# Output projections of the FFNs and of cross attention: the second half as a Strassen pair group

## The chip, the cores and the metric

One core of a Trainium2 chip runs the whole program in one launch. Times are device microseconds of that core, and the kernel's time is the median of several executions. The engines named below are TensorE (PE), which multiplies matrices into PSUM; VectorE (DVE) and ScalarE (ACT), which work on tiles in SBUF and PSUM; GpSimd (POOL); and SyncE (SP), whose queue issues most of the DMAs.

## The reference

One layer of a streaming encoder in float32: 256 tokens, model width 2048, four post-norm blocks.

```python
D_MODEL, SEQ, D_FF, ALPHA = 2048, 256, 5504, 2.0 ** 0.25
def swiglu_ffn(x, w_in, w_out):
    g, u = jnp.split(x @ w_in, 2, axis=-1)
    return (jax.nn.silu(g) * u) @ w_out
...
def memory_cross_attention(h, mem, ...):
    ...
    o = jnp.einsum('bhqk,bkhd->bqhd', p, v).reshape(b, s, D_MODEL)
    return o @ w_xo
...
    h = layer_norm(ALPHA * h + 0.5 * swiglu_ffn(h, ffn1_w_in, ffn1_w_out), ln_ffn1_g, ln_ffn1_b)
    h = layer_norm(ALPHA * h + hybrid_mixer(h, ...), ln_mix_g, ln_mix_b)
    h = layer_norm(ALPHA * h + memory_cross_attention(h, mem, ...), ln_x_g, ln_x_b)
    h = layer_norm(ALPHA * h + 0.5 * swiglu_ffn(h, ffn2_w_in, ffn2_w_out), ln_ffn2_g, ln_ffn2_b)
```

The change touches three of these products, each with 2048 output columns: the two `@ w_out` of the FFNs (K = 5504, 43 tiles of 128) and `@ w_xo` (K = 2048, 16 tiles).

## The kernel before

**Number format.** Every fp32 operand is split into two planes of the type fp32r: `hi` is ScalarE's cast of the number (line 262 for weights), `lo` is what is left of it, subtracted on VectorE (line 265). A product takes three matmuls, hi by hi, hi by lo and lo by hi. The activations stand in SBUF with K on the partitions and are the stationary operand, 128 tokens at a time (a token half, `tt` is 0 or 1); the weights stream through, 512 columns a matmul.

**Weights.** `run()` works through a list of items. Each item has a function that issues matmuls or vector work, and the weights it needs. A weight tile of 2048 columns is 1 MB. It lands by a DMA of SP's queue in one of three `raw` buffers, ScalarE casts it in pieces of 1024 columns, and VectorE makes `lo` with one instruction. The planes go to one of two pairs of buffers ("units") or, where the item has tags, to named blocks of SBUF that happen to be free (X0 to X3, T0 to T3, H0 to H5). An item whose tags end in "early" may be loaded up to five weights ahead, others at most two, and only into a free unit.

**Two ways to multiply.** `out_proj` takes one block of 512 output columns at a time. For a group of four K tiles it issues, for each token half, 4 x 3 matmuls (`mm_tok`, line 296). `pair_group` takes two blocks of 512 columns together, as a 2 by 2 block product for two K tiles at a time: four PSUM tiles `ps[tt, a]`, one for each token half and column block. A plain step (`mm_pair`, line 309) is 2 x 2 x 2 x 3 = 24 matmuls. A step by Strassen's scheme (`mm_sums`, line 363) is seven products instead of eight, 7 x 3 = 21 matmuls. For it VectorE forms four sums of the weights' blocks (`weight_sums`, line 246 with 1024 columns and line 248 twice with 512), their planes take 2048 further columns in two blocks, and the raw tile's own planes need only 1536 of its 2048 columns. Four PSUM tiles `qs` collect products that several results share. At the end of the Strassen steps `shared` (lines 674 to 679) turns `qs` into four tiles in SBUF, which are added to the four results. The sums of the activations (`forms_step`) are kept in blocks named by SUMS_OUT and SUMS_XO and serve every column group.

**Around the change.** The FFN's hidden units are done in two parts of 24 and 19 K tiles (`F_SPLIT`). In the second part the output columns 0 to 1023 are a pair group (`out_pair`, with three Strassen steps, 3, 5 and 7) and the columns 1024 to 2047 are two blocks of `out_proj`, n = 2 and n = 3. The cross output has the same form: one pair group, then `out_proj` for n = 2 and 3. `finish` adds a PSUM tile to the residual `h` (line 749, or 747 with ALPHA) and takes its statistics for the layer norm (`bn_stats`, line 387).

**The skew.** The last four groups of n = 3 run through `skewed`: first all four for token half 0, then the same four, with the weights kept, for token half 1. While TensorE does the second round, the layer norm of half 0 runs on VectorE and ScalarE (`ln_scale`, `ln_T`, lines 392 to 427, 253 and 254), with transposes on TensorE (line 418). The next product starts with half 0 and is skewed likewise, over the layer norm of half 1. At the end of the program `final_steps` takes that place: half 0 is normalized and sent out during the second round, and the last group of half 1 is cut into two parts of 256 columns (`cut`), so that the last statistics wait for little.

**The order.** Instructions are put in order per engine by a scheduler at build time: among those that are ready by its own reckoning, the one that stands earliest in the program goes first, shifted by `prio` (SOON lifts an item by 400 places). On the chip each engine follows this order.

Of the kernel before, what the change touches and what calls it, by code (L numbers as in the profile page):

```python
# [36 lines left out]

AT_XQ = (4, 6), (2, 4, 6)
# [61 lines left out]
class Kernel:  # L100
# [450 lines left out]
    def ffn(self, tag, xT, st, first=None, steps=None, late=None, before=None, tags=None):  # L551
# [6 lines left out]
        for half, nf in enumerate(F_SPLIT):  # L558
# [33 lines left out]
            def out(hid=hid):  # L592
# [50 lines left out]
    def pair_group(self, bank, src, n, nk, x, at, fx, ps, qs, then=None, sums_in=SUM_HOME):  # L643


        steps = -(-nk // 2)
        sums = [c for c in range(steps) if c in at]
        for c in range(steps):
# [14 lines left out]
            def fn(w, c=c, kts=kts):  # L663
                if c == 0:
                    ps.update(self.group_tiles(bank))
                self.mm_pair(ps, w, n, x(), kts, c == 0, c == steps - 1)
# [88 lines left out]
    def out_proj(self, wname, nk, x, scale, st, steps=None, tags=None, n0=0, other=False, cut=False):  # L755
# [5 lines left out]
        groups = [list(range(i, min(i + 4, nk))) for i in range(0, nk, 4)]  # L761

        def finish(tt, n, ps):
            with self.prio(SOON if n == 3 and st is not None else 0):
                self.finish(tt, n, ps, scale, st)

        kept = {}

        def part(n, tts, i, ps, tags=None, held=0, keep=False, again=False):
            grp = groups[i]  # L770

            def fn(w=None):
                if keep:
                    kept[i] = w
                w = kept.pop(i) if again else w
                if cut and again and i == len(groups) - 1:
                    for a in range(2):
                        p = self.mm_tile()
                        self.mm_tok(p[:, :S], 1, w, x(), grp, True, True, a * S, S)
                        hs = h[1][:, n * 512 + a * S:n * 512 + a * S + S]  # L780
                        with self.prio(3 * SOON):
                            nc.vector.tensor_tensor(hs, hs, p[:, :S], ALU.add)
                            nc.vector.bn_stats(st[1][:, 3 + a, :], hs)
                    return
                for tt in tts:
                    if i == 0:
                        ps[tt] = self.at_tile() if other and n == n0 else self.mm_tile()
                    short = cut and again and i == len(groups) - 2
                    self.mm_tok(ps[tt], tt, w, x(), grp, i == 0, short or i == len(groups) - 1)
                    if short:  # L790
                        hs = h[tt][:, n * 512:(n + 1) * 512]
                        with self.prio(3 * SOON):
                            nc.vector.tensor_tensor(hs, hs, ps[tt], ALU.add)
                if i == len(groups) - 1:
                    for tt in tts:
                        finish(tt, n, ps[tt])
            ap = t[wname][n - n0, :, grp[0] * 512:(grp[0] + len(grp)) * 512]
            self.add(fn, *(() if again else ((ap, tags),)), held=held)

        last = len(groups) - 4  # L800
        for n in range(n0, 4):
            ps = {}
            for i in range(len(groups) if n < 3 or steps is None else last):
                part(n, (0, 1), i, ps)
        if steps is not None:
            self.skewed(lambda tt, j, **kw: part(3, (tt,), last + j, ps, **kw), steps(0), tags)
# [620 lines left out]
    def cross(self, xT, st, norm, steps_out):  # L1427
# [343 lines left out]
```

## Time and profile before

| what | value |
|---|---|
| device time, 3 runs | 2434.19 us median, 2432.38 to 2434.53 |
| profiled execution | span 2432.9 us, 29701 instructions; no separate time of it is on the page, its span lies inside the three runs |
| TensorE matmuls | 2423.0 us busy, 11286 instructions |
| TensorE weight loads | 2022.5 us (83%), beside the matmuls |
| VectorE | 2121.1 us (87%) |
| ScalarE | 1551.3 us (64%) |
| GpSimd | 36.1 us (1%) |
| DMA | 516.20 MB, mean 212 GB/s |

A timeline row gives start and duration in microseconds, engine, line, operation, result and operands, and a count of instructions merged into the row; in brackets stands the idle time of the engine before the row and what ended it. Durations of neighbouring instructions overlap a little, so the cost of one in a busy stretch is the distance from its start to the next start. A row of the stretches view gives a window, its length, and for each engine the busy time and in brackets the count.

### The profile page before, as it was taken

How to read it: one execution, taken by the hardware profiler on the slowest of the kernel's cores; microseconds unless marked ns; L12 is line 12 of the kernel's file. 1: busy time of each engine (PE TensorE's matmuls, PEld its weight loads, DVE VectorE, ACT ScalarE, POOL GpSimd, SP SyncE). 2: the span in 40 equal slices, each digit the busy share in tenths (PEclk: the TensorE clock that was granted, in tenths of full speed). 3: DMA queues.
4: the chain of work that ended last, by engine and by line, in shares of the span. 5: the costliest groups of instructions: out<-in, count | busy, mean ns of one | idle time of the engine just before them, and what ended most of it. 6: DMA issues, size and time to landing. Idle time of an engine off the chain costs nothing.

```text
span 2432.9 us, 29701 instructions
## 1 busy us (share of the span) xinstructions
PE 2423.0 (100%) x11286; PEld 2022.5 (83%) x11286; DVE 2121.1 (87%) x2423; ACT 1551.3 (64%) x2017; POOL 36.1 (1%) x81
## 2 busy tenths in 40 slices
PE   9999999999999999999999999999999999999999
PEld 8888888889888888888888888888888888888887
DVE  8999989899878898789788889979879999888997
ACT  6676745666555557878565687765666675556762
POOL 0000000000000001000000000000000000000000
PEclk9999999999999999999999999999999999999999
DMA  7766656666645657776577577655556666666665
GB/s 268 252 214 213 208 199 221 212 199 222 225 172 209 208 209 248 230 209 175 184 249 251 167 236 218 219 184 189 190 199 214 229 221 210 216 208 205 201 223 182
DMA packets 176414, 516.20 MB, mean 212 GB/s; under 512 B 111728, under 2 KB 112496, under 8 KB 121104
## 3 DMA queue, kind: packets, MB, share of 16 engines
q1 hardware_dynamic: 170816, 495.83, 61.2%
q0 software_dynamic: 4592, 17.30, 2.2%
q8 instruction: 88, 1.44, 0.2%
q10 hardware_dynamic: 864, 1.18, 0.1%
q14 instruction: 54, 0.44, 0.1%
HBM read 485.30 MB, written 2.10 MB: 200 GB/s over the span
## 4 chain that ended last, share of the span: by engine, by line
PE 90%; DVE 4%; ACT 3%; DMA 1%; issue 1%; SPq 0%; DVEq 0%; ACTq 0%
PE at L309 24%; PE mm L309 23%; PE mm L296 11%; PE at L363 10%; PE mm L363 10%; PE mm L275 5%; PE mm L277 2%; DVE lo L265 2%; ACT hi L262 1%; PE at L1028 1%; DMA raw<-w_xq 0%; PE at L1499 0%; PE at L1082 0%; PE at L275 0%; DMA raw<-w_o_b 0%
## 5 line engine op out<-in xcount | busy, mean ns | idle before, releaser
L262 ACT CAST hi<-raw 128x1024 fp32r<-128x1024 f32 (+1 forms) x852 | 805.3, 982 | 454.2 <-PE at L309 155.0
L265 DVE TENSOR_TENSOR lo<-raw,hi 128x2048 fp32r<-128x2048 f32 (+1 forms) x427 | 902.3, 2114 | 139.3 <-ACT hi L262 133.4
L309 PE MATMUL mm<-hi,T 128*128 128x512 f32 (+1 forms) x1328 | 311.1, 384 | 1.3 <-DVE v L397 1.3
L309 PEld LDWEIGHTS mm<-hi,T 128*128 128x128 f32 x1328 | 247.3, 188 | 48.5 <-DVE v L397 1.8
L309 PE MATMUL at<-hi,T 128*128 128x512 f32 x1152 | 275.5, 389 | 0.0
L262 ACT CAST X<-H 128x1024 fp32r<-128x1024 f32 (+1 forms) x166 | 170.6, 1034 | 162.0 <-DVE H L246 128.1
L309 PEld LDWEIGHTS at<-hi,T 128*128 128x128 f32 x1152 | 216.2, 188 | 45.1
L265 DVE TENSOR_TENSOR X<-H,X 128x2048 fp32r<-128x2048 f32 (+1 forms) x83 | 186.7, 2250 | 68.6 <-ACT X L262 68.6
L309 PE MATMUL mm<-lo,T 128*128 128x512 f32 (+1 forms) x664 | 160.4, 382 | 0.0
L309 PEld LDWEIGHTS mm<-lo,T 128*128 128x128 f32 x664 | 123.7, 188 | 22.8
L309 PE MATMUL at<-lo,T 128*128 128x512 f32 x576 | 142.4, 389 | 0.0
L309 PE MATMUL at<-hi,H 128*128 128x512 f32 x560 | 133.7, 389 | 0.0
L309 PEld LDWEIGHTS at<-lo,T 128*128 128x128 f32 x576 | 108.1, 188 | 22.5
L309 PEld LDWEIGHTS at<-hi,H 128*128 128x128 f32 x560 | 104.9, 188 | 21.6
L309 PE MATMUL mm<-hi,H 128*128 128x512 f32 x480 | 115.5, 391 | 0.3 <-DVE w L679 0.3
L248 DVE TENSOR_TENSOR H<-H,raw 128x512 f32<-128x512 f32 (+1 forms) x166 | 112.2, 676 | 2.2
L309 PEld LDWEIGHTS mm<-hi,H 128*128 128x128 f32 x480 | 89.5, 188 | 19.3 <-DVE w L679 0.8
L246 DVE TENSOR_TENSOR H<-raw 128x1024 f32<-128x1024 f32 (+1 forms) x83 | 99.4, 1198 | 0.9 <-DMA raw<-w_gate 0.8
L363 PE MATMUL mm<-X,X 128*128 128x512 f32 x342 | 91.1, 392 | 0.0
L262 ACT CAST X<-raw 128x1024 fp32r<-128x1024 f32 (+1 forms) x54 | 55.4, 1036 | 48.7 <-DVE raw L248 38.7
L363 PE MATMUL at<-X,X 128*128 128x512 f32 (+1 forms) x315 | 82.5, 386 | 0.9 <-DVE X L265 0.5
L849 ACT COPY w<-w 128x1024 uint16<-128x1024 uint16 (+1 forms) x60 | 75.8, 1276 | 0.6 <-DMA w<-w 0.5
(373 smaller groups left out, 4123.1 us busy)
## 6 DMA issues: line engine op xcount, KB each, us to landing
raw<-ffn_w_in SPq DMA_DIRECT2D x150, 1024.0 KB, 4.8
raw<-ffn_w_out SPq DMA_DIRECT2D x66, 1024.0 KB, 4.8
raw<-w_gate SPq DMA_DIRECT2D x32, 1024.0 KB, 4.8
raw<-ffn_w_out_r SPq DMA_DIRECT2D x16, 1024.0 KB, 4.9
raw<-w_qk SPq DMA_DIRECT2D x16, 1024.0 KB, 5.5
raw<-w_o_b SPq DMA_DIRECT2D x16, 1024.0 KB, 4.8
raw<-w_out SPq DMA_DIRECT2D x16, 1024.0 KB, 5.2
raw<-w_xk SPq DMA_DIRECT2D x16, 1024.0 KB, 5.3
```

Source lines behind the costliest of these rows:

```text
L246: self.nc.vector.tensor_tensor(two[0], two[1], raw[:, :m].unsqueeze(1).to_broadcast([P, 2, m]), ALU.add)
L248: self.nc.vector.tensor_tensor(t[:, a * m:a * m + m], t[:, b * m:b * m + m], raw[:, a * m:a * m + m], ALU.add)
L262: self.last_hi = self.nc.scalar.copy(hi[:, c:d], src[:, c:d])
L265: self.last_lo = self.nc.vector.tensor_tensor(lo[:, :n], src, hi[:, :n].bitcast(F32), ALU.subtract)
L275: self.nc.tensor.matmul(ps, hi[j], x.both(kt), start=(j == 0), stop=False)
L277: self.last_mm = self.nc.tensor.matmul(ps[:, :S], lo[j], x.at(0, kt), start=False, stop=(j == n - 1))
L296: self.last_mm = self.nc.tensor.matmul(ps, x.at(xi, kt)[:, tt * P:(tt + 1) * P], w[wi][:, j * 512 + c:j * 512 + c + m], start=(start and j ...
L309: self.last_mm = self.nc.tensor.matmul(ps[tt, g][:, :n], x.at(xi, kt)[:, tt * P:(tt + 1) * P], w[wi][:, c:c + n], start=first and j + wi + ...
L363: self.last_mm = self.nc.tensor.matmul(bank[:, :m], a[xi], v[wi][:, c * m:(c + 1) * m], start=own and first and wi + xi == 0, stop=own and ...
L849: self.nc.scalar.copy(self.words(u, n).rearrange("p (c k) -> p k c", k=2), self.words(s, n).rearrange("p (k c) -> p k c", k=2))
L1028: nc.tensor.matmul(ps[:, c0:c0 + nk], q[:, tt * P:(tt + 1) * P], k[:, :nk], start=(j == 0), stop=(j == len(parts) - 1))
```

## The change

The columns 1024 to 2047 of the three outputs become a second pair group for a part of the K tiles, with steps in a given order. The last eight K tiles of it stay out of the pair group: for them `out_skew` adds matmuls of the `out_proj` kind onto the same four PSUM tiles, token half 0 first (both column blocks), then token half 1. In the FFNs the order of steps is 6, 3, 8, 5, 9, 7, of which 3, 5 and 7 are Strassen steps and 9 has one K tile. In the cross output it is 0, 4, 2, 6 with 4 and 6 by Strassen. The sums of the activations that the first group used are used again. Weights are laid out to match on the host, with the same number of bytes.

The skew's four weight tiles in the cross output go to other blocks: H0 and H1, X0 and X1, T2 and T3, and T0 and T1, the last of them without "early"; before they went to T0 and T1, T2 and T3, H0 and H1, H2 and H3. In the final steps the gain of the third column block of token half 1 is applied after that block's `finish` (`self.tail`) instead of ahead of the second round.

```diff
+OUT_ORDER, OUT_ENDS = (6, 3, 8, 5, 9, 7), (0, 1, 2, 3, 4, 5, 8, 9)
+AT_XO, XO_ORDER, XO_ENDS = (4, 6), (0, 4, 2, 6), (2, 3, 6, 7, 10, 11, 14, 15)
...
-                    self.out_proj(tag + "_w_out_r", nf, x, False, st, steps, tags, 2, cut=tags is None)
+                    self.out_skew(bank ^ 1, src[1], tag + "_w_out_r", nf, OUT_ORDER, OUT_ENDS, x, homes, fh, False, st, steps,
+                                  tags, tags is None, SUM_HOME + ("H5",))
...
-    def pair_group(self, bank, src, n, nk, x, at, fx, ps, qs, then=None, sums_in=SUM_HOME):
+    def pair_group(self, bank, src, n, nk, x, at, fx, ps, qs, then=None, sums_in=SUM_HOME, order=None, open_end=False):
...
+        order = range(-(-nk // 2)) if order is None else order
+        sums = [c for c in order if c in at]
+        for i, c in enumerate(order):
...
-    def out_proj(self, wname, nk, x, scale, st, steps=None, tags=None, n0=0, other=False, cut=False):
+    def out_skew(self, bank, src, wname, nk, order, ends, x, at, fx, scale, st, steps, tags=None, cut=False,
+                 sums_in=SUM_HOME):
+        nc, t, h = self.nc, self.t, self.h
+        ps, qs, kept = {}, {}, {}
+
+        def shared():
+            for (tt, a), s in qs["add"].items():
+                hs = h[tt][:, (2 + a) * 512:(3 + a) * 512]
+                if scale:
+                    nc.vector.scalar_tensor_tensor(hs, hs, ALPHA, s, ALU.mult, ALU.add)
+                else:
+                    nc.vector.tensor_tensor(hs, hs, s, ALU.add)
+
+        def part(tt, j, tags=None, held=0, keep=False, again=False):
+            a, i = divmod(j, 2)
+            grp = ends[4 * i:4 * i + 4]
+
+            def fn(w=None):
+                if keep:
+                    kept[j] = w
+                w = kept.pop(j) if again else w
+                n, p = 2 + a, ps[tt, a]
+                if cut and tt and a and i:
+                    for b in range(2):
+                        p = self.mm_tile()
+                        self.mm_tok(p[:, :S], 1, w, x(), grp, True, True, b * S, S)
...
+                short = cut and tt and a
+                self.mm_tok(p, tt, w, x(), grp, False, short or i == 1)
...
+                elif i:
+                    with self.prio(SOON):
+                        self.finish(tt, n, p, False, st)
+                        if cut and tt:
+                            self.tail()
+            ap = t[wname][a, :, 2048 * i:2048 * i + 2048]
+            self.add(fn, *(() if again else ((ap, tags),)), held=held)
+
+        self.pair_group(bank, src, 512, nk, x, at, fx, ps, qs, shared, sums_in, order, True)
+        self.skewed(part, steps(0), tags)
...
-            self.out_proj("w_xo_r", KT, x, True, st, steps_out, (
-                ("T0", "T1", "early"), ("T2", "T3", "early"), ("H0", "H1", "early"), ("H2", "H3", "early")), 2)
+            self.out_skew(0, t["w_xo"][1], "w_xo_r", KT, XO_ORDER, XO_ENDS, x, AT_XO, fx, True, st, steps_out, (
+                ("H0", "H1", "early"), ("X0", "X1", "early"), ("T2", "T3", "early"), ("T0", "T1")), sums_in=(("T0", "T1"),))
...
-            for q in range(3):
-                hs = h[1][:, q * 512:(q + 1) * 512]
-                nc.vector.tensor_tensor(hs, hs, e["gb"][0][:, q * 512:(q + 1) * 512], ALU.mult)
+            for q in range(2):
+                gain(q)
+            self.tail = lambda: gain(2)
```

More of the change, by code (lines that the diff above doesn't have):

```diff
@@ L772, in fn @@
             def fn(w=None):
                 if keep:
[L774 to L777, printed above, removed]
+                    kept[j] = w
[3 more added lines that the diff above has]
+                    for b in range(2):
                         p = self.mm_tile()
-                        self.mm_tok(p[:, :S], 1, w, x(), grp, True, True, a * S, S)
-                        hs = h[1][:, n * 512 + a * S:n * 512 + a * S + S]
+                        self.mm_tok(p[:, :S], 1, w, x(), grp, True, True, b * S, S)
+                        hs = h[1][:, n * 512 + b * S:n * 512 + b * S + S]
@@ L781, in fn @@
                         with self.prio(3 * SOON):
                             nc.vector.tensor_tensor(hs, hs, p[:, :S], ALU.add)
-                            nc.vector.bn_stats(st[1][:, 3 + a, :], hs)
+                            nc.vector.bn_stats(st[1][:, 3 + b, :], hs)
                     return
[L785 to L797, printed above, removed]
-            self.add(fn, *(() if again else ((ap, tags),)), held=held)
[L800 to L806, printed above, removed]
+                short = cut and tt and a
```

32 lines of the change are left out of this document (16 added, 16 removed).

## The prediction

> **What bounds the kernel now.** I read the page's first two parts, then its chain, then the timelines of TensorE and VectorE around the three places, and last the busy time by stretches there.
>
> ```profile
> PE 2423.0 (100%) x11286; PEld 2022.5 (83%) x11286; DVE 2121.1 (87%) x2423; ACT 1551.3 (64%) x2017; POOL 36.1 (1%) x81
> PE 90%; DVE 4%; ACT 3%; DMA 1%; issue 1%; SPq 0%; DVEq 0%; ACTq 0%
> ```
>
> TensorE is the bound: it holds 90% of the chain that ended last and hardly ever waits. VectorE is second with 87%, an average over stages, so the question is how much of its 13% lies where the change puts work.
>
> ```profile
> 601.44 3.79 PE L309 MATMUL at<-hi,H 128*128 128x512 f32 x16
> ...
> 606.88 0.62 PE L363 MATMUL at<-hi,H 128*128 128x512 f32 x2
> ...
> 611.64 3.79 PE L309 MATMUL at<-hi,H 128*128 128x512 f32 x16
> ```
>
> This is the first FFN's existing pair group. A plain step starts at 601.44 and the next, a Strassen step, at 606.88: 24 matmuls in 5.44 us, 0.2267 us each. The Strassen step ends at 611.64: 21 matmuls in 4.76 us. One Strassen step is worth 0.68 us of TensorE, if nothing else changes.
>
> **TensorE's saving.** In each FFN n = 2 and 3 are 19 K tiles x 2 halves x 2 blocks x 3 = 228 matmuls. After: steps 24 + 21 + 24 + 21 + 12 + 21 = 123, and 8 x 2 x 2 x 3 = 96 for the last eight K tiles, 219 together. In the cross output 192 become 24 + 21 + 24 + 21 + 96 = 186. So 9 + 9 + 6 = 24 matmuls go, 24 x 0.2267 = 5.44 us (2.04, 2.04 and 1.36).
>
> The Trainium skill, TensorE: Matmul & The Clock Gate, Part 1, puts a warm matmul of 512 columns at about 215.7 ns; by that the saving would be an estimated 5.18 us. The rows say 226.7 ns at a granted clock of 1.00, and they decide.
>
> The second half-round is 48 matmuls after (two blocks x 8 K tiles x 3) and 45 or 48 before, so the cover over the layer norm of half 0 stays about 10.9 us. In the last product the cut group has four K tiles instead of three.
>
> ```profile
> 2418.21 5.04 PE L296 MATMUL mm<-X,H 128*128 128x512 f32 x30
> 2423.08 1.02 PE L1607 MATMUL mm<-h,ident 128*128 128x512 f32 x2
> ```
>
> The 30 are 12 of 512 columns (2.72 us) and 18 of 256, which leaves 2.15 us, 0.12 us each, so two halves cost about one whole and the longer cut is free to within 0.1 us.
>
> **What VectorE pays for a Strassen step.**
>
> ```profile
> 607.37 2.29 DVE L265 TENSOR_TENSOR X<-H,X 128x2048 fp32r<-128x2048 f32 x1 [1.12 <-ACT X L262]
> 609.58 2.28 DVE L265 TENSOR_TENSOR lo<-raw,hi 128x2048 fp32r<-128x2048 f32 x1
> 611.78 1.22 DVE L246 TENSOR_TENSOR H<-raw 128x1024 f32<-128x1024 f32 x1
> 612.91 1.75 DVE L265 TENSOR_TENSOR lo<-raw,hi 128x1536 fp32r<-128x1536 f32 x1
> 614.58 0.68 DVE L248 TENSOR_TENSOR H<-H,raw 128x512 f32<-128x512 f32 x1
> 615.18 0.55 DVE L254 TENSOR_TENSOR H<-w,H 128x384 fp32r<-128x384 f32 x1
> ```
>
> From start to start: `lo` of a plain tile 2.20 us; a Strassen step takes 2.21 (`lo` of the sums) + 1.13 (first sum) + 1.67 (`lo` of 1536 columns) + 2 x 0.60 (two more sums) = 6.2 us. Extra: 4.0 us of VectorE for 0.68 us of TensorE. ScalarE pays 1536 more columns, one and a half casts of about 1 us; with 64% busy I cost that at nothing, and without the slack it would be 12 us over eight steps.
>
> ```profile
> 621.91 0.68 DVE L676 TENSOR_TENSOR w<-w,mm 128x512 f32<-128x512 f32 x1
> 622.51 1.22 DVE L265 TENSOR_TENSOR lo<-raw,hi 128x1024 fp32r<-128x1024 f32 x1
> 623.64 0.69 DVE L677 TENSOR_TENSOR w<-w,w 128x512 f32<-128x512 f32 x1
> 624.25 0.68 DVE L628 TENSOR_TENSOR h<-h,w 128x512 f32<-128x512 f32 x1
> ...
> 627.85 2.29 DVE L265 TENSOR_TENSOR lo<-raw,hi 128x2048 fp32r<-128x2048 f32 x1
> 630.05 1.28 DVE L749 TENSOR_TENSOR h<-h,at 128x512 f32<-128x512 f32 x2
> ```
>
> Each new group also runs `shared` and its four additions to `h`: eight instructions at 0.60 to 0.62 us, 4.9 us. `finish` keeps its four additions and four statistics, only later. So VectorE gets 3 x 4.0 + 4.9 = 16.9 us in each FFN, 2 x 4.0 + 4.9 = 12.9 us in the cross output, 46.7 us in all.
>
> **Where that lands.** A weight can be prepared only one or two steps ahead: two units, three raw buffers, one home for the sums. So I take stretches that begin where VectorE has become continuously busy ahead of the place, and end where its work was last due.
>
> ```profile
> core 0: us, PE busy (x) PEld busy (x) DVE busy (x) ACT busy (x) POOL busy (x), PEclk, DMA share, GB/s
> 617.50:697.20 79.70, 79.00 (x365) 65.31 (x363) 64.44 (x83) 41.80 (x56) 0.00 (x0) 1.00 0.60 212
> 1675.30:1757.20 81.90, 81.90 (x378) 67.79 (x377) 73.36 (x96) 48.02 (x62) 0.00 (x0) 1.00 0.57 206
> 2359.00:2423.00 64.00, 64.00 (x292) 53.32 (x292) 50.41 (x59) 21.87 (x24) 0.00 (x0) 1.00 0.57 201
> 710.00:731.00 21.00, 21.00 (x94) 17.41 (x93) 11.38 (x15) 9.20 (x12) 0.16 (x1) 1.00 0.61 207
> ```
>
> FFN 1: VectorE has 64.44 of 79.70 us to do and gets 16.9 more: 81.3 us, so the stretch ends at least 1.6 us later than now, while TensorE alone would end 2.04 us earlier. Cross: 73.36 + 12.9 = 86.3 us in a stretch of 81.90, 4.4 us later. FFN 2: 50.41 + 16.9 = 67.3 us against 64.00, 3.3 us later. The ends are real due times:
>
> ```profile
> 695.89 1.29 DVE L254 TENSOR_TENSOR T<-w,T 128x512 fp32r<-128x512 f32 x2 [0.25 <-ACT T L253]
> 697.16 2.07 PE L296 MATMUL mm<-hi,T 128*128 128x512 f32 x8
> 1755.31 1.29 DVE L254 TENSOR_TENSOR T<-w,T 128x512 fp32r<-128x512 f32 x2 [0.25 <-ACT T L253]
> 1756.55 2.09 PE L296 MATMUL mm<-hi,T 128*128 128x512 f32 x8
> ```
>
> In both stretches the normalized half 1 is finished by VectorE just as TensorE starts on it; there is no lead left to spend. What VectorE did early inside the stretches (three of the next product's weights, 2.2 us each) is still due inside them.
>
> **FFN 2's end.**
>
> ```profile
> 2414.42 0.26 DVE L392 BATCH_NORM_AGGREGATE mv<-bn 128x2 f32<-128x24 f32 x1
> 2418.99 2.73 DVE L1596 SCALAR_TENSOR_TENSOR h<-h,y,T 128x512 f32<-128x512 f32 x4
> 2421.64 0.68 DVE L793 TENSOR_TENSOR h<-h,mm 128x512 f32<-128x512 f32 x1
> ```
>
> The norm of half 0 keeps VectorE busy from 2414.42 to 2421.64, when the last chain begins. `finish` of half 1's third block and its gain (two instructions of 0.6 us, one statistic) move into that time; they are no new work and count in the 64 us, but push the same chain.
>
> **Smaller edits.** The first Strassen step now comes second in its group, and its `qs` tiles are the PSUM that `finish` of the first group must empty: in FFN 1 the additions started at 630.05, and TensorE would want the tiles from 635.44 + 4 x 0.2267 = 636.3 on. Behind 6.2 us for the step's own weights they come up to 2.5 us late; bound 0 to 2.5 us a place. I take 0 on top, since VectorE works on meanwhile and the sum above already counts that work. In the cross output the layer norm writes T0, which the last weight tile now holds until 4 matmuls (0.9 us) before the round's end: bound 0 to 1.2 us (a cast and a subtraction of 512 columns, 0.6 us each). I take 0, because VectorE's backlog reaches that point later anyway; without the backlog it would be the 1.2 us. SP's queue issues the same bytes. In the cross output a Strassen step holds two of the three raw buffers, so a load starts later by up to its landing time:
>
> ```profile
> raw<-ffn_w_out SPq DMA_DIRECT2D x66, 1024.0 KB, 4.8
> ```
>
> With 4.8 us to land against 5.44 us a step this is bounded by 0 and about 2 us; I take 0, covered by the same backlog.
>
> **Sum.** 1.6 + 4.4 + 3.3 = +9.3 us, TensorE's 5.44 us being lost in waits for VectorE. The span of the profiled execution is 2432.9 us and the median 2434.19, 1.3 us above; on the median 2434.2 + 9.3 = 2443.5, I say 2443.
>
> **Rivals.**
>
> *The saving arrives.* VectorE carries its backlog out of the stretches into time where it is free: from 710 to 731 it is busy 11.38 of 21 us. Then 2434.2 - 5.4 = 2428.8, with a few tenths of waits 2429. It needs the norms' instructions to pass the carried weights without delaying them. Against it: the carried weights are those TensorE wants next. It decides if less than 0.6 us of the three overruns stays.
>
> *The FFNs come out as TensorE alone would have it, the cross output overruns.* In FFN 1 only 1.6 us are missing, and at the end some output work of half 0 can slide behind the last chain. -2.04 - 2.04 + 4.4 = +0.3: 2434.5.
>
> *The free time cannot be filled.* The three stretches have 15.3 + 8.5 + 13.6 = 37.4 us free. Part is latency: 1.12 us before line 265 above wait for ScalarE's cast. If a quarter stays free: 9.3 + 9.3 = +18.6, 2453; with a sixth, 2449.5.
>
> *TensorE slows down after long waits.* Its longest waits now are short, and the granted clock is 1.00 in all four stretches.
>
> ```profile
> PE mm L309 <- DVE v L397: 1.3, 1, 1.3
> ```
>
> If each overrun stood in one piece and matmuls ran at half rate for as long as the longest of them, 4.4 us, each place would lose 2.2 us more: 9.3 + 6.6 = +15.9, 2450. The Trainium skill, TensorE: Matmul & The Clock Gate, Part 1, has such a rule: an idle window of about 3.4 us halves the clock until it has been busy as long again. By it, an estimated 1.7 us is lost at a place; no row here shows a wait that long.
>
> **How the numbers follow.** A measurement of this kernel can tell about 0.2%, 4.9 us, from no change: 2429.3 and 2439.1 are the bounds. Chances: the sum 0.50 (its own range 2438 to 2448), the saving 0.12, the mixed case 0.25, unfilled time 0.10, the slow clock 0.03. The time is that of the likeliest, 2443. The range reaches from the saving, 2429.5, to unfilled time, 2453. Faster 0.10 (most of the saving's case), same 0.30 (the mixed case and edges of its neighbours), slower 0.60.
>
> **What would show it.** Right: 24 fewer matmuls and 2.04, 1.36 and 2.04 us less of TensorE's own time; VectorE busy above 97% from the first group's end through the layer norm at all three places, with about 47 us more in total; TensorE waiting there for line 265, line 749 or the norm's lines; the first `mm<-hi,T` on half 1 some 2 us later than now in FFN 1 and 4 us in cross. Wrong: VectorE with several free microseconds in those stretches while TensorE runs through; or weights prepared before the stretches begin, which the buffers should prevent.

## The result, and the profile after

| | median us | lowest to highest | runs |
|---|---|---|---|
| before | 2434.36 | 2432.38 to 2434.87 | 4 |
| after | 2464.36 | 2463.99 to 2465.01 | 4 |

The ratio is 1.0125, with a 95% interval of 1.0113 to 1.0137: 30 us slower, where 9 were forecast. The span of the profiled execution went from 2432.9 to 2462.2 us. Line numbers are two to six higher than before (296 became 298, 265 became 267, 418 became 420, 410 became 412, 1611 became 1617). First the engines and the chain on the page of after:

```profile
PE 2428.9 (99%) x11265; PEld 2021.4 (82%) x11265; DVE 2164.6 (88%) x2479; ACT 1564.9 (64%) x2037; POOL 35.9 (1%) x81
PE 86%; DVE 6%; ACT 3%; DMA 3%; issue 2%; SPq 0%; DVEq 0%; ACTq 0%
```

TensorE has 21 matmul records less, 24 for the Strassen steps and three more because the cut group splits 12 matmuls in two instead of 9. It is nevertheless 5.9 us busier: some of its work ran slower. VectorE has 43.5 us more, close to the 46.7 forecast. TensorE's share of the chain fell from 90% to 86%. What it waits for, by the waits of TensorE (total, times, longest):

```profile
PE at L420 <- DVE h L412: 6.8, 1, 6.8
PE at L420 <- issue: 5.8, 1, 5.8
PE mm L1617 <- ACT w L1615: 5.3, 1, 5.3
PE mm L298 <- DVE T L256: 2.5, 2, 2.2
PE mm L298 <- ACT T L255: 1.9, 2, 1.2
```

Three single long waits, one a place: in front of the transposes of half 0 in cross and in FFN 1, and in front of the program's last six matmuls. The timeline of VectorE in FFN 1 shows what happened ahead of the second:

```profile
678.55 0.24 DVE L394 BATCH_NORM_AGGREGATE mv<-bn 128x2 f32<-128x24 f32 x1
...
679.32 2.28 DVE L267 TENSOR_TENSOR lo<-raw,hi 128x2048 fp32r<-128x2048 f32 x1
681.51 0.14 DVE L374 TENSOR_SCALAR y<-v 128x1 int32<-128x1 int32 x1
682.13 0.69 DVE L752 TENSOR_TENSOR h<-h,mm 128x512 f32<-128x512 f32 x1 [0.47 <-PE mm L298]
...
683.82 2.23 DVE L267 TENSOR_TENSOR H<-raw,H 128x2048 fp32r<-128x2048 f32 x1
...
687.20 1.00 DVE L412 TENSOR_SCALAR h<-h,mv,y 128x512 f32<-128x512 f32 x2
```

Before, the same norm ran in one piece, by VectorE's timeline:

```profile
677.44 0.26 DVE L392 BATCH_NORM_AGGREGATE mv<-bn 128x2 f32<-128x24 f32 x1
...
679.86 1.00 DVE L410 TENSOR_SCALAR h<-h,mv,y 128x512 f32<-128x512 f32 x2
```

The aggregate is 1.1 us later, but from it to the scaling of half 0 it takes 8.65 us instead of 2.42: two remainders (`lo`) of the next product's weights and half 1's own additions and statistics stand between the norm's nine tiny, dependent instructions. Before, TensorE's transposes stood within its second round, in FFN 1 and in cross:

```profile
680.50 1.06 PE L418 MATMUL at<-ident,h 128*128 128x128 f32 x8 [0.70 <-issue]
...
1739.44 1.03 PE L418 MATMUL at<-ident,h 128*128 128x128 f32 x8
```

TensorE's timeline after:

```profile
687.84 3.46 PE L420 MATMUL at<-ident,h 128*128 128x128 f32 x16 [5.75 <-issue]
...
1758.83 3.67 PE L420 MATMUL at<-ident,h 128*128 128x128 f32 x16 [6.78 <-DVE h L412]
...
1765.86 3.12 PE L298 MATMUL mm<-hi,T 128*128 128x512 f32 x7 [2.24 <-DVE T L256]
...
2446.59 1.02 PE L1613 MATMUL mm<-h,ident 128*128 128x512 f32 x2
2452.95 2.08 PE L1617 MATMUL mm<-T,w 128*128 128x512 f32 x2 [5.34 <-ACT w L1615]
2454.82 1.92 PE L1617 MATMUL at<-T,w 128*128 128x512 f32 x2
2456.53 1.91 PE L1617 MATMUL mm<-T,w 128*128 128x512 f32 x2
```

Behind each long wait the same instructions are slow: a pair of 512 columns 1.9 to 2.1 us instead of 1.02. The stretches of after (window, length, busy time by engine, then the granted clock) show both:

```profile
617.99:705.73 87.74, 79.81 (x355) 64.51 (x354) 80.33 (x103) 47.02 (x63) 0.00 (x0) 0.96 0.55 197
1684.00:1779.90 95.90, 85.21 (x371) 68.54 (x369) 84.67 (x112) 51.27 (x68) 0.00 (x0) 0.95 0.52 178
2381.40:2446.00 64.60, 64.37 (x290) 52.16 (x290) 62.06 (x67) 27.50 (x31) 0.00 (x0) 1.00 0.51 186
```

VectorE's work came out as summed in FFN 1 (80.33 against 81.3 us) and in cross (84.67 against 86.3), yet it stands free there for 7.4 and 11.2 us. In FFN 2 it is 62.06 against 67.3: the end of half 0's norm, some 5 us of VectorE's work, now falls behind the stretch (its last row stood at 2418.99 before):

```profile
2443.53 0.26 DVE L394 BATCH_NORM_AGGREGATE mv<-bn 128x2 f32<-128x24 f32 x1
...
2449.34 2.73 DVE L1602 SCALAR_TENSOR_TENSOR h<-h,y,T 128x512 f32<-128x512 f32 x4
```

A finer cut in FFN 1:

```profile
680.00:690.00 10.00, 4.25 (x20) 3.58 (x19) 9.39 (x26) 2.90 (x5) 0.00 (x0) 0.71 0.62 215
690.00:700.00 10.00, 8.54 (x38) 6.85 (x38) 7.97 (x14) 7.45 (x15) 0.00 (x0) 0.95 0.01 5
```

The granted clock falls to 0.71 in the stretch with the wait of 5.75 us; in the 3.46 us of the transposes behind it it is 0.55, and 0.50 in cross's 3.67 us and in the last six matmuls. The Trainium skill, TensorE: Matmul & The Clock Gate, Part 1, says that an idle window of about 3.4 us halves the clock; this trace agrees for its three waits of 5.3 to 6.8 us.

To place the loss I use three marks: the first matmul on the normalized half 1 in FFN 1 (697.16 us before) and in cross (1756.55), and the end (2432.9). From mark to mark, after against before: FFN 1 +8.6, cross +14.8, FFN 2 +5.9, together 29.3 us. In FFN 1 the transposes start 7.3 us late (680.50 before) and the way from there to the mark takes 1.2 us more. In cross that is 10.8 and 4.0. In FFN 2 the last product ends 1.6 us *earlier* by the marks (2444.87 against 2423.08, with 23.4 us brought along), so TensorE's saving of 2.04 us nearly arrives, and the tail behind it takes 17.3 us instead of 9.8.

### The profile page after: what moved, and what is told of

It reads as the page before. It is cut to its first block, busy times and chain, and to the rows that moved or that the text cites. A ratio compares the mean times of both kernels' runs of the same rounds, so it can differ in the third digit from the quotient of the medians.

```text
span 2462.2 us, 29751 instructions
## 1 busy us (share of the span) xinstructions
PE 2428.9 (99%) x11265; PEld 2021.4 (82%) x11265; DVE 2164.6 (88%) x2479; ACT 1564.9 (64%) x2037; POOL 35.9 (1%) x81
## 4 chain that ended last, share of the span: by engine, by line
PE 86%; DVE 6%; ACT 3%; DMA 3%; issue 2%; SPq 0%; DVEq 0%; ACTq 0%
PE at L311 25%; PE mm L311 24%; PE at L365 11%; PE mm L365 11%; PE mm L298 6%; PE mm L277 5%; PE mm L279 2%; DVE lo L267 2%; ACT hi L264 1%; PE at L1030 1%; DMA raw<-w_xq 1%; DMA raw<-w_xv 0%; PE at L1501 0%; PE at L1084 0%; PE at L277 0%
## 5 line engine op out<-in xcount | busy, mean ns | idle before, releaser
L264 ACT CAST X<-H 128x1024 fp32r<-128x1024 f32 (+1 forms) x178 | 183.2, 1035 | 164.3 <-DVE H L248 128.6
L267 DVE TENSOR_TENSOR X<-H,X 128x2048 fp32r<-128x2048 f32 (+1 forms) x89 | 200.5, 2253 | 71.6 <-ACT X L264 71.6
L311 PE MATMUL mm<-hi,H 128*128 128x512 f32 x592 | 143.7, 391 | 0.4 <-DVE w L682 0.4
L311 PEld LDWEIGHTS mm<-hi,H 128*128 128x128 f32 x592 | 110.6, 188 | 23.7 <-DVE w L682 0.8
L250 DVE TENSOR_TENSOR H<-H,raw 128x512 f32<-128x512 f32 (+1 forms) x178 | 120.7, 678 | 2.3
L248 DVE TENSOR_TENSOR H<-raw 128x1024 f32<-128x1024 f32 (+1 forms) x89 | 106.8, 1200 | 1.4 <-DMA raw<-w_gate 1.0
L365 PE MATMUL at<-X,X 128*128 128x512 f32 (+1 forms) x369 | 98.0, 388 | 1.3 <-DVE X L267 0.7
L264 ACT CAST X<-raw 128x1024 fp32r<-128x1024 f32 x56 | 58.2, 1052 | 47.5 <-DVE raw L250 38.9
L365 PEld LDWEIGHTS at<-X,X 128*128 128x128 f32 x369 | 67.7, 188 | 17.9 <-DVE X L267 2.9
```

What stands on the lines that cost most here:

```text
L248: self.nc.vector.tensor_tensor(two[0], two[1], raw[:, :m].unsqueeze(1).to_broadcast([P, 2, m]), ALU.add)
L250: self.nc.vector.tensor_tensor(t[:, a * m:a * m + m], t[:, b * m:b * m + m], raw[:, a * m:a * m + m], ALU.add)
L264: self.last_hi = self.nc.scalar.copy(hi[:, c:d], src[:, c:d])
L267: self.last_lo = self.nc.vector.tensor_tensor(lo[:, :n], src, hi[:, :n].bitcast(F32), ALU.subtract)
L311: self.last_mm = self.nc.tensor.matmul(ps[tt, g][:, :n], x.at(xi, kt)[:, tt * P:(tt + 1) * P], w[wi][:, c:c + n], start=first and j + wi + ...
L365: self.last_mm = self.nc.tensor.matmul(bank[:, :m], a[xi], v[wi][:, c * m:(c + 1) * m], start=own and first and wi + xi == 0, stop=own and ...
```

## The experiments

The theories, by the letters of the expectations: A, VectorE has more to do than fits, and its backlog is the cause; B, the new form itself costs; C, the skew is lost because TensorE takes half 1's first products ahead of half 0's last; D, half 0's norm is cut open by the next product's weights; E, TensorE runs at half rate after a long wait. The table gives all runs; the last three columns are microseconds lost against before from mark to mark in the one profiled execution.

| kernel | median us | ratio, 95% interval | FFN 1 | cross | FFN 2 |
|---|---|---|---|---|---|
| after | 2464.36 | 1.0113 to 1.0137 | 8.6 | 14.8 | 5.9 |
| plain | 2437.28 | 1.0001 to 1.0019 | -0.1 | 2.8 | 1.2 |
| order | 2462.81 | 1.0097 to 1.0128 | 8.6 | 12.0 | 7.2 |
| hold | 2451.66 | 1.0048 to 1.0082 | 4.0 | 8.7 | 5.8 |
| warm | 2467.39 | 1.0117 to 1.0148 | 10.5 | 16.8 | 5.4 |
| homes | 2453.16 | 1.0062 to 1.0089 | 3.1 | 10.4 | 5.7 |
| hold_pool | 2463.09 | 1.0104 to 1.0132 | 9.3 | 13.4 | 7.6 |
| warm3 | 2462.39 | 1.0102 to 1.0129 | 9.6 | 12.1 | 5.9 |
| end | 2462.85 | 1.0102 to 1.0130 | 8.5 | 14.6 | 4.1 |
| light | 2442.59 | 1.0023 to 1.0051 | -0.8 | 9.4 | -0.4 |
| one_early | 2445.51 | 1.0037 to 1.0063 | 1.7 | 4.9 | 1.7 |
| one_late | 2445.97 | 1.0036 to 1.0064 | 2.0 | 10.3 | 1.9 |
| plain_load | 2469.83 | 1.0129 to 1.0160 | 14.5 | 13.6 | 7.8 |
| light_hold | 2438.98 | 1.0010 to 1.0027 | -0.3 | 4.9 | 0.9 |

**plain: the new form without its Strassen steps.**

```diff
-        self.pair_group(bank, src, 512, nk, x, at, fx, ps, qs, shared, sums_in, order, True)
+        self.pair_group(bank, src, 512, nk, x, (), fx, ps, qs, shared, sums_in, order, True)
...
-                        self.finish(tt, n, p, False, st)
+                        self.finish(tt, n, p, scale, st)
...
```

> The second groups keep the new form (two column blocks together, the given order of steps, eight K tiles by token halves, the new blocks for weights), but none of their steps goes by Strassen: 24 matmuls more, and VectorE loses the extra 46.7 us. Theory A (VectorE's extra work and what it holds up is the whole cause): back to the time before, 2434 us within 3 us, the layer norm of half 0 again inside the second half-round. Theory B (the form itself costs, for instance the blocks given to the last weights or the first group's PSUM wanted one step earlier): stays above 2445 us.

2437.28 us, at the edge of what A expected. The pair group, the order of K, the new blocks and the later `finish` cost about 0.1% (0.2% at most), most of it in cross; 27 of the 30 us belong to the Strassen steps.

**order: TensorE must finish half 0's products first.**

```diff
+                with self.tc.issue_after(kept["last"].ins) if tt else nullcontext():
                     self.mm_tok(p, tt, w, x(), grp, False, short or i == 1)
+                if not tt:
+                    kept["last"] = self.last_mm
```

> As the changed kernel, but TensorE must do all of token half 0's last matmuls before half 1's. In the changed kernel 17 to 24 of half 1's matmuls went ahead in each place because the last two weights of half 0 came late, so the norm of half 0 had about 7 us of matmuls over it instead of 10.9. Theory C (the lost skew is what costs): the cover is back, 10 us or more gained, about 2452 us. Theory A (VectorE is behind whatever TensorE does first): the wait only moves ahead, 2464 us within 3 us.

2462.81 us: the same. TensorE now waits for half 0's last weights (5.2 us at the longest, at line 267's remainder) and less for the norm. Theory C falls: TensorE's order was a consequence of late weights, not a cause. The transposes show something else here, by TensorE's timeline:

```profile
688.77 1.94 PE L420 MATMUL at<-ident,h 128*128 128x128 f32 x16 [1.58 <-issue]
...
1758.26 1.97 PE L420 MATMUL at<-ident,h 128*128 128x128 f32 x16 [2.88 <-DVE h L412]
```

In after the same transposes take 3.46 and 3.67 us. Here the granted clock is 1.00, and they follow the first scaling of `h` as closely as there (0.65 and 0.59 us behind it, against 0.64 and 0.60).

**hold: the next product's weights are prepared only behind half 0's norm** (FFN 1 and cross).

```diff
-            while nxt < len(queue) and ahead(need, held):
+            passed += fn is Kernel.wall
+            while nxt < len(queue) and (nxt < need or walls[nxt] <= passed) and ahead(need, held):
...
-        self.skewed(part, steps(0), tags)
+        first, *rest = steps(0)
+        self.skewed(part, [first if cut else first + [Kernel.wall], *rest], tags)
```

> As the changed kernel, but in FFN 1 and the cross output the next product's weights are loaded only once the norm of half 0 has been put into the program, so VectorE's subtractions for them stand behind that norm's chain. Same work, same matmuls. Theory D (the norm's chain of small instructions is cut open by two subtractions of 2.2 us, and TensorE waits for its end): the waits of 5.8 and 6.8 us in front of the transposes shrink to 1 or 2 us, with the slow clock behind them, about 2448 us. Theory A (the sum of VectorE's work decides): the same work comes later and TensorE waits for the weights instead, 2464 us within 4 us.

2451.66 us, 12.7 less than after. In FFN 1 the transposes stand inside the round again, by TensorE's timeline of this kernel, but the next weights are now late themselves:

```profile
680.44 0.63 PE L429 MATMUL at<-ident,h 128*128 128x128 f32 x4
...
691.05 1.20 PE L307 MATMUL mm<-lo,T 128*128 128x512 f32 x4 [0.61 <-DVE lo L276]
...
695.75 1.21 PE L307 MATMUL mm<-H,T 128*128 128x512 f32 x4 [1.67 <-DVE H L276]
```

So the early work on the next weights costs 4.5 us in FFN 1 and about 6 in cross, and putting it off turns a part of the loss into waits for the work put off, as A would have it. The cut norm is not all of the gain: from aggregate to scaling the norm takes 3.4 us in both places (8.7 and 8.5 in after), but the aggregate itself also comes 2.2 us (FFN 1) and 6.6 us (cross) sooner than in after.

**warm and warm3: 24 useless matmuls where TensorE would wait.** In warm the scheduler put them behind the transposes; in warm3 they write the tile of the first transposes and so stand in front of them; the norm's later steps also move behind the round.

```diff
+            if (tt, q) == (0, 0) and ln in ("ln_ffn1", "ln_x"):
+                x = self.warm_of[ln]()
+                with self.tc.issue_after(self.last_mm.ins):
+                    for _ in range(24):
+                        self.nc.tensor.matmul(ps, x.at(0, 0)[:, :P], x.both(0), start=True, stop=True)
...
```

> As the changed kernel, with 24 matmuls of 512 columns (5.4 us) of no use put behind the last matmul of FFN 1's and of the cross output's second half-round, where TensorE waits 5.8 and 6.8 us. Theory E (part of the loss is TensorE at half rate after a wait longer than some 3.4 us): the granted clock stays at 1.0 there, the 16 transposes take 1.6 us again instead of 3.5 and 3.7, and 4 to 5 us are gained in the two places, about 2459 us. If the clock costs nothing beside the wait: 2464 us or, where the extra matmuls outlast the wait, a little more.

> 24 useless matmuls of 512 columns (5.4 us) on TensorE between the last matmul of half 1 and the first transposes of half 0, in FFN 1 and in cross, so that TensorE does not stand still there. Theory E (TensorE runs at half rate after a wait of more than some 3 us): the 16 transposes take 1.6 us again instead of 3.46 and 3.67 and cross's next matmuls their 0.2267 us each; -1.9 and -3.8 us, less what the dummies overhang (up to 0.5 us in FFN 1): 2458.5 to 2460. Rival (the transposes are slow because each waits for VectorE's or ScalarE's next quarter of h): same time, 2464 to 2465, and the transposes stay at 3.4 us.

warm, 2467.39 us, tells nothing on the clock: the waits of 3.6 and 6.1 us stayed in front of the transposes, which stayed slow. warm3, TensorE's timeline:

```profile
681.91 5.61 PE L420 MATMUL at<-H 128*128 128x512 f32 x24
687.36 1.91 PE L425 MATMUL at<-ident,h 128*128 128x128 f32 x16
692.35 3.83 PE L298 MATMUL mm<-hi,T 128*128 128x512 f32 x8 [3.08 <-ACT T L255]
```

The transposes take 1.91 us instead of 3.46. Here their input was ready 2.2 us sooner (the scaling stands at 684.98, since one remainder left the norm), so this row alone doesn't refute the rival, that each transpose waits for its quarter; the two rows of order do, and with them and the granted clocks E is shown. But the next matmuls start at 692.35 against 692.53, since the work of VectorE and ScalarE behind the transposes is hardly sooner, and the wait of 3.08 us in front of them slows the next eight (3.83 us at a granted clock of 0.56; 1.98 at full rate). The gain is 2 us of the 4 to 6 expected: 2.7 in cross, and a loss of 1 in FFN 1.

**homes: half 0's last weights in blocks that no Strassen sum holds.**

```diff
-                                  tags, tags is None, SUM_HOME + ("H5",))
+                                  tags or (None, None, ("T2", "T3", "next"), ("X2", "X3", "next")), tags is None,
+                                  SUM_HOME + ("H5",))
...
-            ("T0", "T1", "early"), ("T2", "T3", "early"), ("X0", "X1", "early"), ("X2", "X3", "early")))
+            None, None, ("T0", "T1", "early"), ("T2", "T3", "early")))
...
-                ("H0", "H1", "early"), ("X0", "X1", "early"), ("T2", "T3", "early"), ("T0", "T1")), sums_in=(("T0", "T1"),))
+                ("H0", "H1", "early"), ("X0", "X1", "early"), ("T2", "T3", "early"), None), sums_in=(("T0", "T1"),))
```

> The last two weights of half 0 go into blocks that no Strassen sum holds (FFN 1: T instead of X; FFN 2: T2/T3 instead of X0/X1; cross: a unit instead of T0/T1), and two of the next product's weights lose their early place. Theory D (the norm of half 0 is cut open by the next product's weights): the next weights find no unit free before the round's end, so the norm runs uncut as in the kernel with held weights, -4.5 us in FFN 1 and -6 to -8 in cross; with half 0 done sooner in FFN 2 too, some -2: 2450 to 2453. Theory A (VectorE has more to do than the stretch holds, in whatever order): the same work is due at the same end, 2461 to 2465.

2453.16 us, at the upper end of what D says: 5.5 us less in FFN 1 and 4.4 in cross, where a wait of 4.0 us follows the transposes. In FFN 2 the last weight stayed in a block of the sums (X2, X3), and its loss stayed too.

**end: half 0's last instructions behind half 1's mean in the program's tail.**

```diff
-                    mean, r, nm = self.ln_scale(st[tt], lambda nm: got.update(v=centre(nm)))
+                    def mid(nm):
+                        got.update(v=centre(nm))
+                        with self.tc.issue_after(e["mean"].ins):
+                            for q in (3, 0, 1, 2):
+                                put(0, q * 512, 512, h[0][:, q * 512:(q + 1) * 512], e["r"])
+                    mean, r, nm = self.ln_scale(st[tt], mid)
...
```

> FFN 2's last chain: the four last instructions on half 0 (2.73 us on VectorE, line 1602) go behind the mean of half 1 instead of ahead of it, so that TensorE's last six matmuls get their input earlier. If the order on VectorE and the slow clock set the loss here: the wait of 5.34 us falls to about 2.3, the six matmuls take 1.02 a pair instead of 1.92, and the end comes 2.5 to 3 us earlier: 2461.5. If only the amount of VectorE's work counts (theory A): 2464, the same 2.73 us being done later in the same chain.

2462.85 us, 1.5 below after, the intervals overlapping; in the profile the tail is 1.7 us shorter. TensorE's timeline:

```profile
2449.70 2.08 PE L1617 MATMUL mm<-T,w 128*128 128x512 f32 x2 [2.36 <-ACT w L1615]
2451.57 1.64 PE L1617 MATMUL at<-T,w 128*128 128x512 f32 x2
2453.04 1.02 PE L1617 MATMUL mm<-T,w 128*128 128x512 f32 x2
```

The wait fell as expected, the rate did not recover at once: the first pair is slow behind 2.36 us too. Half 0's four instructions now stand in half 1's chain, so more than half of the gain was given back; the time lies between the two expectations.

**hold_pool: hold, with the weights' sums and the FFNs' additions to `h` on GpSimd.**

```diff
-        self.nc.vector.tensor_tensor(two[0], two[1],
+        eng.tensor_tensor(two[0], two[1],
...
-                    nc.vector.tensor_tensor(hs, hs, s, ALU.add)
+                    nc.gpsimd.tensor_tensor(hs, hs, s, ALU.add)
```

> Next weights held back as before, and in addition the raw sums of the second groups' Strassen steps (about 2.3 us a step of VectorE) and, in the FFNs, the additions of shared to h (2.4 us) on GpSimd: VectorE loses about 9.5 us of work in each FFN and 4.7 in cross. Theory A for what is left (the overrun that the prediction counted): FFN 1's remaining 4 us and FFN 2's go, cross's 6 to 7 halve: 2440 to 2444 from 2451.7, and if TensorE's own saving then shows, down to 2436. Rival: what is left are latency chains and the slow clock after waits, which the amount of VectorE work does not set: 2449 to 2452.

2463.09 us, 11.4 *more* than hold: both expectations missed. The groups of GpSimd in FFN 1 (busy, then mean ns):

```profile
L260 POOL TENSOR_TENSOR H<-raw 128x1024 f32<-128x1024 f32 x3 | 12.0, 4011 | 635.6 <-DMA raw<-ffn_w_out 632.1 <-DVE X L279 3.5
L262 POOL TENSOR_TENSOR H<-H,raw 128x512 f32<-128x512 f32 x6 | 9.1, 1520 | 0.5
L787 POOL TENSOR_TENSOR h<-h,w 128x512 f32<-128x512 f32 x4 | 8.1, 2062 | 10.1 <-DVE w L694 5.6 <-ACT w L691 4.5
```

The first sum of a step takes 4.0 us in the mean where VectorE needs 1.22, and ScalarE's cast, VectorE's remainder and the matmuls wait for it in turn. It says nothing on A; light and plain_load do.

**light: the Strassen steps without their remainders.**

```diff
             self.last_hi = self.nc.scalar.copy(hi[:, c:d], src[:, c:d])
+        if light:
+            return hi, hi
...
```

> The Strassen steps of the second groups use the rounded weights twice instead of weights and remainders, so VectorE doesn't form the remainders (left out of the computation: `lo` of these steps, 2.21 + 1.67 us each); TensorE, ScalarE, loads, homes and order of the products stay. A Strassen step then costs VectorE 2.3 us, as much as a plain step's `lo`, and only the 4.9 us for shared and its additions stay extra: 69 of 79.7 us in FFN 1, 78 of 81.9 in cross, 55 of 64 in FFN 2. Theory A (VectorE's backlog, not the places where weights live, makes half 0 late, cuts the norm open and lays it bare): the loss goes at all three places and most of TensorE's 5.4 us shows: 2432 to 2438. Rival (homes held until the last Strassen step, and next weights queued in the norm, whatever VectorE's load): at most the 4 us of the hold kernel's rest go: 2450 to 2460.

2442.59 us, above A's range and well below the rival's: 22 of the 30 us go with 30 us of VectorE's work (2134.5 us busy against 2164.6), no other work being left out. FFN 1 and FFN 2 come out faster than before (-0.8, -0.4). Cross stays 9.4 us behind. VectorE's timeline there:

```profile
1735.35 0.26 DVE L397 BATCH_NORM_AGGREGATE mv<-bn 128x2 f32<-128x24 f32 x1
1735.52 2.23 DVE L270 TENSOR_TENSOR lo<-raw,hi 128x2048 fp32r<-128x2048 f32 x1
...
1738.38 2.28 DVE L270 TENSOR_TENSOR X<-raw,X 128x2048 fp32r<-128x2048 f32 x1
...
1743.72 1.00 DVE L415 TENSOR_SCALAR h<-h,mv,y 128x512 f32<-128x512 f32 x2
```

The norm is cut open again, 8.4 us from aggregate to scaling, though VectorE's sum (78 of 81.9 us) left it room.

**light_hold: light and hold together.**

> The kernel that leaves out the remainders of the Strassen steps (2442.6), with the next product's weights held back behind half 0's norm as well. What is left there is mostly cross, where the trace shows two remainders of the next weights (2.23 and 2.28 us) inside half 0's norm (8.4 us from the aggregate to the first scaling, 2.4 before), a wait of 3.3 us and slow matmuls behind it. If VectorE's load and the cut norm together are the whole loss: the norm is whole again and 5 to 8 us go, 2434.5 to 2438. If something else costs time in cross (TensorE's own order, homes): 2441 to 2444.

2438.98 us, a little above the range expected. Cross's norm takes 2.4 us again (1733.01 to 1735.44) and its transposes stand in the round; 4.9 us stay, with a wait on the next product:

```profile
1749.76 2.48 PE L310 MATMUL mm<-hi,T 128*128 128x512 f32 x7 [1.76 <-DVE T L266]
```

There a weight's remainder of 2.28 us (1746.64) sits in half 1's norm, in front of the T that TensorE wants.

**plain_load: plain, and VectorE's extra work alone.**

```diff
+            if extra:
+                for m in (1664, n):
+                    self.last_lo = self.nc.vector.tensor_tensor(lo[:, :m], src[:, :m], hi[:, :m].bitcast(F32), ALU.subtract)
...
+    def idle_adds(self):
+        for i in range(8):
+            v = self.w2()
+            hs = self.h[0][:, :512] if i < 4 else self.h[1][:, :512]
+            with self.tc.issue_after(self.last_lo.ins):
+                self.nc.vector.tensor_tensor(v, hs, hs, ALU.add)
```

> The kernel without Strassen steps in the second groups (2437.3: the same matmuls as before the change, last weights where they were) with VectorE's extra work alone: `lo` of the three (cross: two) K pairs formed once and another 4.0 us' worth of it again (1664 and 2048 columns), and eight useless additions of 512 columns (4.9 us) behind the group. No home is held longer, no sum is formed, ScalarE and TensorE do what they did. If VectorE's extra work alone makes half 0's last weights late and lets the next weights into the norm: most of the loss comes back, 2455 to 2468. If the homes held by the sums, ScalarE's extra casts or the new order of TensorE are needed for it: 2437 to 2446.

2469.83 us, 32.6 above plain and a little above the range expected. The page of this kernel shows VectorE as busy as in after (2164.8 against 2164.6 us), ScalarE as in plain:

```profile
PE 2435.8 (99%) x11289; PEld 2029.0 (82%) x11289; DVE 2164.8 (88%) x2463; ACT 1553.3 (63%) x2015; POOL 36.2 (1%) x81
```

and in FFN 1 the same cut norm (7.5 us from aggregate to scaling), the same long wait and the same slow transposes:

```profile
683.96 0.25 DVE L397 BATCH_NORM_AGGREGATE mv<-bn 128x2 f32<-128x24 f32 x1
684.12 2.23 DVE L267 TENSOR_TENSOR lo<-raw,hi 128x2048 fp32r<-128x2048 f32 x1
686.33 2.29 DVE L267 TENSOR_TENSOR H<-raw,H 128x2048 fp32r<-128x2048 f32 x1
...
691.45 1.00 DVE L415 TENSOR_SCALAR h<-h,mv,y 128x512 f32<-128x512 f32 x2
```

```profile
692.09 3.42 PE L423 MATMUL at<-ident,h 128*128 128x128 f32 x16 [5.81 <-issue]
```

No sum, no longer held home, no Strassen product and no extra cast of ScalarE is needed for the loss: VectorE's work alone opens the norm. (Its extra remainders are due ahead of the matmuls of their own K pair, which costs 9.4 us more in five waits at line 270; after has no such waits, so the 32.6 us are not a measure of size.)

**one_early and one_late: one Strassen step a place, as second or as last step.**

```diff
+        at = [c for c in at if c == (4 if scale else 3)]
         self.pair_group(bank, src, 512, nk, x, at, fx, ps, qs, shared, sums_in, order, True)
```

(In one_late 6 and 7 stand for 4 and 3.)

> One Strassen step in each second group, the second step of the group (line 3 of K pairs in the FFNs, 4 in cross); the others plain, the matmuls they save come back. VectorE gets 8.9 us more in each place instead of 16.9 and 12.9: 73.3 of 79.7, 82.3 of 81.9, 59.3 of 64. Theory A: no overrun in the FFNs, 0.4 us in cross; from the kernel without Strassen steps (2437.3) minus 3 x 0.68 plus 0.4: 2435 to 2437. Rival (any Strassen step breaks the skew): a third to a half of the loss stays, 2445 to 2452.

> The same with one Strassen step as the last step of each second group, just ahead of the round on token halves. Same work for all engines as with the early one. If only the amount of VectorE's work counts: 2435 to 2437 again. If what counts is how much of it is due in the last steps ahead of the norm (6.2 us for a step of 4.76 us, shared and four additions behind it, and the sums' home held until then): half 0's last weights come some 5 to 9 us later, and the time is 2442 to 2450.

2445.51 and 2445.97 us. one_early lies 8.5 us above what A expected and in the range of the rival, but the skew isn't broken there: the transposes of half 0 stand inside the round in FFN 1 (680.99) as before. 8.9 us of extra work fit into the stretch by the sum, but not where they fall. TensorE's timeline has one wait of about 2 us in each place, at the plain step behind the Strassen step, the first of them:

```profile
646.40 2.11 PE L311 MATMUL mm<-lo,H 128*128 128x512 f32 x8 [2.18 <-DVE lo L267]
```

`finish` of the first group, the step's own weights and `shared` all come due within two steps there. one_late has no such wait; most of its loss is in cross, in front of the transposes (a wait of 3.1 us for `h`, then 16 transposes in 3.62 us). The marks of one_early come from an execution of 2443.03 us, so they show some 2 us less than the median.

## Why the prediction was wrong

Its direction was right; its size was not, 9 us against 30, and its range ended at 2453.

*TensorE's saving*, 5.4 us: in line with the records and with light's FFNs, 0.4 to 0.8 us under before. light_hold, without most of VectorE's extra work, still isn't faster than before (1.0010 to 1.0027), so little of it shows even then.

*VectorE's extra work*, 46.7 us: right in kind (43.5), and plain_load and light together show that it is the cause. ScalarE's extra casts, put at nothing, came to 13.6 us, and plain_load has the loss without them.

*Where it lands: the step that failed.* "81.3 us, so the stretch ends at least 1.6 us later than now" takes VectorE's free time for fillable and lets the end of the stretch slip by the overrun alone. The work was sized right, but the stretch is not one queue with one due time. First, the extra work is due ahead of half 0's last products, so it is half 0 that is late: in FFN 2 the norm's aggregate came 8.7 us ahead of the last chain before (2414.42, 2423.08) and 1.3 ahead after (2443.53, 2444.87). "The cover over the layer norm of half 0 stays about 10.9 us" failed with it. Second, instructions of 2.2 us that VectorE had done early now get into the gaps of a chain of nine instructions of 0.15 to 0.3 us, each of which needs the one before; hold, which keeps them behind the whole norm, gives 12.7 us back. Third, with the norm bare TensorE stands still, and VectorE and ScalarE then pass the half back and forth, so that VectorE stands idle in part (7.4 and 11.2 us in the whole stretches). So the sign that the prediction gave for itself, VectorE busy above 97%, did not come: the three stretches show 92, 88 and 96%. The rival "the free time cannot be filled", 2453 at 0.10, named the symptom and 18.6 us of the 30.

*The slow clock*, a rival at 0.03, showed itself at all three places. From the rows above, against the rates of full speed: transposes 3.46 and 3.67 us for 1.91, seven matmuls 3.12 for the 1.88 of hold's timeline, the last six 5.9 for 3.1. That is 7.4 us of slower matmuls beside a loss of 29, and not all of it counts: in warm3 transposes at full rate brought FFN 1's next matmuls only 0.2 us forward. The prediction took its longest wait for 4.4 us, and the waits were 5.3 to 6.8.

*Smaller edits at 0.* `finish` behind the first Strassen step cost TensorE nothing in FFN 1 of after (no wait from 630 to 664). In one_early a wait of 2.2 us follows the Strassen step, but it is for a weight's remainder behind `finish` and `shared`, not for those tiles. The later loads and the layer norm's wait for T0 in cross were not isolated. In cross the new form alone cost 2.8 us.

*FFN 2's end*: the place was right ("push the same chain"), the size 7.5 us in the tail against 3.3, 2.8 of it the slow clock.

What stays open: how cross's 14.8 us divide. Light takes off 5.4, holding the weights 6.1, both together 9.9, and the new form alone costs 2.8; the rest, some 2 us, wasn't followed further. No version here beats the kernel before: plain is nearest, and light_hold, which leaves work out, bounds what better placing of the rest could give.

## What to carry to other kernels

Sum the work of the second engine by due time, not by stretch: ask what is due before the latency chain begins, and whether that chain's cover shrinks. An engine at 88% that feeds the bound engine through a chain of tiny dependent instructions is full well before its sum says so, because any long instruction that it can no longer do early can land inside the chain. A wait of TensorE that grows past two or three microseconds should be priced with slow matmuls behind it as a likely extra: here waits of 2.36 and 3.08 us brought them, one of 2.88 us didn't.

## What the runs showed of the hardware

- TensorE slowed behind waits shorter than the rule cited above suggests: a pair took 2.08 us behind 2.36 us (in end), eight matmuls 3.83 behind 3.08 (in warm3). Length alone doesn't decide: behind 2.88 us in order 16 transposes ran at full rate, as matmuls did behind 1.07 us in hold. The same part of the Trainium skill says that the window runs freely and isn't reset when a kernel starts. That alone doesn't account for 2.36 us, which is less than the window it states, and no run here isolates what does.
- GpSimd's sums of 1024 columns in FFN 1 of hold_pool took 5.25, 3.82 and 2.97 us, VectorE's 1.22. Its pairs of sums of 512 columns took 2.65, 2.65 and 4.05 us. Of VectorE's three remainders of 1536 columns there, two took 1.75 us, as in hold, and the one beside the pair of 4.05 us took 2.20. The Trainium skill, GPSIMD Engine Reference, section 1, says that GpSimd's SBUF interfaces are shared with VectorE, with contention from VectorE's instructions that have two SBUF inputs. That slow pair agrees; the sum of 3.82 us stood beside a remainder of 1.75 us, so VectorE did not always pay.
